# Streaming-encoder block on one core: embedding blocks at three stage borders, a gate unit moved ahead of attention, and attention's last pair handed over in SBUF

## The chip, the cores and the metric

The kernel runs on one core of one Trainium2 chip. The metric is the time of one execution in device microseconds (us). The engines of a core have their own instruction queues, each worked through in order: PE (TensorE, the matmuls; its weight loads are listed as PEld), DVE (VectorE, elementwise), ACT (ScalarE, activation functions and copies), POOL (GpSimd) and SP (SyncE). SP, POOL and ACT also issue DMA transfers; these are listed as SPq, POOLq and ACTq.

## The reference

One layer of an encoder over 512 tokens of width 2048, in float32:

```python
h = rms_norm(x)
q_a, k_a, v_a, q_g, k_g, v_g, r_g, gate_lr = split(h @ w_in)        # 2048 -> 6160
y_a = chunked_band_attention(q_a, k_a, v_a, bias)                   # 16 heads of 64
o_g = rms_norm(gated_linear_attention(q_g, k_g, v_g, log_a(gate_lr)))   # 4 heads, value width 256
x = x + concat(y_a, o_g * silu(r_g)) @ w_out                        # 2048 -> 2048
h = rms_norm(x)
u_gate, u_val = split(causal_conv3(h @ w_ffn_up))                   # 2048 -> 2 x 5632
x = x + (gelu(u_gate) * u_val) @ w_ffn_down
h = rms_norm(x)
x = x + sigmoid(h @ w_ple_gate) * (p @ w_ple_proj)                  # p: 512 x 256 embeddings
return rms_norm(x)
```

## The kernel before

Each large matrix product is made with seven block products in place of eight (P1 to P7, a fast matrix multiplication with sums of weight blocks and sums of input blocks). A **unit** is one piece of such a product: 256 output columns, 512 tokens. A block product is 24 matmuls of 128 x 128 x 256: every operand is split into a high and a low part, and high x high, high x low and low x high are added up in PSUM. The high part of a weight block is a copy on ACT, the low part a subtraction on DVE (`prep_high`, `prep_low`, tile `wsplit`); both are issued two products ahead of their use. After each product `collect` takes the result out of PSUM, on ACT for the first product of a quarter of the unit's output and on DVE otherwise.

The **stages** run one after the other: `linear` (units 16 to 19 are the four heads of linear attention, 20 to 23 the attention's values, 8 a gate unit), `front` (units 0 to 7 are pairs of attention heads, 9, 10 and 11 the other gate units), `embed` (four blocks of p @ w_ple_proj), `wo` (x @ w_out), `up`, `dn0` to `dn2` (the down projection in three parts) and `pg` (the gate of the embeddings). `wo`, `up` and `pg` begin and end with two units side by side, so that their products alternate. A step is one product; an embedding block is one step too, of 24 matmuls with 512 columns (`embedding`, L722). It goes through four PSUM results from auxiliary banks (`psum_aux`; four such banks at first, two from `more_banks` on), which ACT copies into two pages `pp_o`; the ACT queue stores each page, 512 KB, to the scratch `ppd`. The gate stage reads it back hundreds of steps later (`load_gate`).

The order of the work on PE, DVE and ACT is written out by hand. The list `agenda` holds for every step what is to be issued there, with a key: 0 ahead of everything, 1 between the high and the low part of the coming weights, above 1 behind the matmuls of the step. What a unit's output needs after its last product is such a list as well (`attend`, `after_gates`, `gla_head`: pairs of step and key, counted from the step behind the unit). These instructions stay in program order on their engines, so an instruction that waits holds up all behind it.

A stage's input operands lie in SBUF in seven forms (R11, R21, R22, N1, T3, N2, T4), each in two tiles of four blocks (`g` 0 and 1). They come from scratch in DRAM (`store_pair` writes them, `Stage.load` reads them) and are split again. The last two blocks of a **chained** stage come straight from SBUF, as `tails`: for `wo` those of gate units 10 and 11, for `up` and `pg` those of the last two units of the stage before.

Raw weights are loaded into pages of 512 KB. `free` lists the free ones and `wanted` the blocks to come, in order; `issue` gives free pages to wanted blocks, oldest page first. A name with a star is a page that the kernel will write itself: `issue` leaves one page free for it and goes on; `made_page` takes it. `release` puts a page back and calls `issue` at once. S blocks are sums: SP loads one block and POOL adds the other with an accumulating DMA. Other pages have fixed tags and turn in small rings (`page`): `c` (c0, and later c1, c2, c0), `x` (r6, later x0 and x1), `u`. Page r7 holds in turn the output of a linear head (`og`) and then the attention's bias.

Linear attention's own tiles (pool `gla`) and the attention's (pool `att`) share space: `open_attention` closes the first and opens the second, nine steps after unit 0 begins. `attention_done` opens the pool `late`, gives three more pages to the weights, and switches the rings; it comes 19 steps after unit 7 begins.

Of the kernel before, what the change touches and what calls it, by code (L numbers as in the profile page):

```python
# [43 lines left out]
def encoder_block(ctx: ExitStack, tc: tile.TileContext, A, out):  # L44
# [677 lines left out]
    def embedding(unit):  # L722

        hi, lo = unit.w["PP"]
        for i in range(4):
            if i % 2 == 0:
                spare = {(0, 2): (pg, "u0"), (1, 2): (late[0], "u3")}.get((unit.u, i))
                o = (spare[0].tile([P, 1024], F32, tag=spare[1], name="pp_o") if spare else page("c", "pp_o")).rearrange("p (s t) -> p s t", s=2)
            pp = psum_aux("pp")
            for k in range(2):  # L730
                w = slice((i * 2 + k) * P, (i * 2 + k + 1) * P)
                product3(pp, hi[:, w], lo[:, w], ps_[0][:, k], k == 0, k == 1)
            act.activation(o[:, i % 2, :], pp, AF.Copy)
            if i % 2:
                m = 4 * unit.u + i - 1
                nc.scalar.dma_start(ppd[m % 8:m % 8 + 2, m // 8].rearrange("m p t -> p m t"), o)

# [5 lines left out]
    def attend(unit):  # L743
# [97 lines left out]
        if b % 2:  # L841
            items.append((12, 1, lambda: store_pair(mixd, b // 2, ypair[0][:, 0, :], ypair[0][:, 1, :])))
# [220 lines left out]
    def front_weights(u, q):  # L1063
# [3 lines left out]
        if u >= 16:  # L1067
# [4 lines left out]
    linear = Stage("in", [16, 20, 21, 17, 22, 23, 18, 8, 19], 8, None, front_weights, front_after, "own", "own", single=True,  # L1072
                   groups=((0,), (1, 2), (3,), (4, 5), (6,), (7,), (8,)))
    front = Stage("in", [0, 1, 2, 3, 4, 5, 6, 7, 9, 10, 11], 8, None, front_weights, front_after, "dma", "dma", single=True)
# [8 lines left out]
    embed = Stage("pp", [0, 1, 2, 3], 8, None, lambda u, q: A["w_ple_proj"][u], lambda u: [], "dma", "dma", single=True)  # L1083
    for u in embed.units:
# [13 lines left out]
    units = [u for st in stages for u in st.units]  # L1098
    steps = []
    base = {}  # L1100
    for st in stages:
        for group in st.groups:
# [4 lines left out]
            need = [[(u, name) for name in (NEEDS[u.sums] if u.stage is not embed else ("L11",))] for u in group]  # L1107
# [47 lines left out]
    agenda[i0 + 2].append((0, lambda: raws.update(p=embedding_load(page("c", "pT")))))  # L1155
# [16 lines left out]
    agenda[i0 + 11].append((0, more_banks))  # L1172
# [169 lines left out]
    agenda[base[front.units[0]] + 9].append((1.5, open_attention))  # L1342
# [138 lines left out]
def _layout(x, p, norm_mix_w, w_in, att_rel_bias, w_gla_gate_up, b_gla_gate, gla_norm_w,  # L1481
# [16 lines left out]
        "w_out": _blocks(w_out[0].reshape(8, 2, P, D).transpose(1, 0, 2, 3).reshape(D, D)),  # L1498
# [31 lines left out]
```

## Time and profile before

| what | value |
|---|---|
| median of 3 runs | 2252.64 us (2250.53 to 2253.16) |
| the profiled execution | 2254.49 us |
| its span on the core | 2252.8 us |
| mean granted TensorE clock | 0.993 |
| matmuls | 18588 |
| DMA moved | 518.31 MB |

The span is the time from the first to the last instruction of the profiled execution; some time lies around it. In a row of the timeline stand the start and the length in us, the engine, the line, the operation, the tile written and the tiles read, the shape, the number of such instructions merged, and in brackets the idle time of the engine before it with what ended it. Because a helper records most instructions, their line is L64, and they are told apart by their tiles: `wsplit` is a split weight, `accA` to `accC` are PSUM results of products, `u` a unit's output, `pp_o` and `pp` an embedding block's page and PSUM result, `in_`, `wo_`, `up_`, `dn_` and `pg_` with R, N or T the operands of the stages. DMA rows show the issue; a transfer's time to landing is listed apart.

### The profile page before, as it was taken

The numbers are of one execution on the slowest core, as the hardware profiler recorded it, in microseconds if no ns is written. First come the engines' busy times: TensorE is split into PE (matmuls) and PEld (weight loads), VectorE is DVE, ScalarE is ACT, GpSimd is POOL, SyncE is SP. The second block draws the span as 40 slices with busy tenths as digits, with TensorE's granted clock in tenths as the row PEclk, the third lists the DMA queues.
The fourth block names the chain that finished last, engine by engine and source line by source line (L and its number), as shares of the span: only waits on it lengthen the run. The fifth ranks groups of instructions, "written<-read, shape, count | busy, mean of one in ns | idle before, by whom it ended". The sixth has DMA issues, their size and how long they took to land.

```text
span 2252.8 us, 46290 instructions
## 1 busy us (share of the span) xinstructions
PE 2196.4 (97%) x18588; PEld 2146.3 (95%) x18588; DVE 1937.3 (86%) x2655; ACT 1344.6 (60%) x2000; POOL 158.6 (7%) x196
## 2 busy tenths in 40 slices
PE   9999998999999999999999999999999999999995
PEld 7899988999989999999999999999999999999995
DVE  8476778999879898999889888988898797999997
ACT  9455556777666665555555555555564554667655
POOL 0000000000000100000000001000000100000000
PEclk9999999999999999999999999999999999999998
DMA  6466755667888987888888888888876967879894
GB/s 238 134 181 193 214 160 150 180 189 199 287 268 278 315 235 207 224 229 218 221 218 223 211 225 216 222 218 213 256 237 232 314 229 260 299 252 336 264 307 152
DMA packets 190760, 518.31 MB, mean 230 GB/s; under 512 B 20272, under 2 KB 66608, under 8 KB 190544
## 3 DMA queue, kind: packets, MB, share of 16 engines
q1 hardware_dynamic: 160272, 415.72, 54.2%
q0 software_dynamic: 25920, 93.33, 23.2%
q10 hardware_dynamic: 4352, 6.29, 0.8%
q8 instruction: 146, 2.39, 0.4%
q14 instruction: 70, 0.57, 0.1%
HBM read 441.86 MB, written 71.30 MB: 228 GB/s over the span
## 4 chain that ended last, share of the span: by engine, by line
PE 80%; DVE 9%; DMA 4%; ACT 4%; issue 2%; ACTq 0%; SPq 0%; DVEq 0%
PE accA L64 41%; PE accC L64 21%; PE accB L64 10%; DVE wsplit L64 3%; PE v L240 1%; PE v L239 1%; PE v L241 1%; ACT wsplit L64 1%; DVE u L64 1%; DMA dn_R<-g_R 1%; PE py L64 1%; PE ptr L64 1%; PE psc L64 1%; DMA ppd<-pp_o 1%; DVE l L64 1%
## 5 line engine op out<-in xcount | busy, mean ns | idle before, releaser
L64 ACT ACTIVATE wsplit<-l 128x1024 fp32r<-128x1024 f32 (+1 forms) x476 | 495.7, 1042 | 292.0 <-PE accC L64 123.6
L64 DVE TENSOR_TENSOR wsplit<-l,wsplit 128x1024 fp32r<-128x1024 f32 (+1 forms) x476 | 570.5, 1200 | 114.7 <-ACT wsplit L64 113.3
L64 DVE TENSOR_TENSOR wsplit<-s,wsplit 128x1024 fp32r<-128x1024 f32 (+1 forms) x253 | 303.4, 1200 | 58.2 <-ACT wsplit L64 57.7
L64 ACT ACTIVATE wsplit<-s 128x1024 fp32r<-128x1024 f32 (+1 forms) x253 | 262.7, 1039 | 64.0 <-PE accB L64 36.1
L64 ACT ACTIVATE u<-accA 128x256 f32<-128x256 f32 x302 | 114.2, 378 | 268.9 <-PE accA L64 268.9
L64 PE MATMUL accA<-up_T,wsplit 128*128 128x256 f32 x2112 | 253.6, 276 | 0.4 <-ACT wsplit L64 0.4
L64 PEld LDWEIGHTS accA<-up_T,wsplit 128*128 128x128 f32 x2112 | 245.8, 188 | 0.7 <-ACT wsplit L64 0.6
L64 DVE SCALAR_TENSOR_TENSOR cv<-u,cw,cv 128x511 f32<-128x511 f32 (+1 forms) x176 | 131.5, 747 | 3.1
L405 POOL DMA_DIRECT2D s<-in_w_up x88 | 76.2, 866 | 764.2 <-DMA s<-in_w_up 280.9
L64 PE MATMUL accA<-up_N,wsplit 128*128 128x256 f32 x1056 | 127.1, 276 | 1.3 <-DVE wsplit L64 1.3
L64 PE MATMUL accA<-dn_T,wsplit 128*128 128x256 f32 x1056 | 126.2, 276 | 2.0 <-DVE wsplit L64 1.7
L64 PE MATMUL accC<-up_N,wsplit 128*128 128x256 f32 x1056 | 126.8, 276 | 0.9 <-DVE wsplit L64 0.9
L64 PE MATMUL accB<-up_R,wsplit 128*128 128x256 f32 x1056 | 126.8, 276 | 0.6 <-DVE wsplit L64 0.6
L64 PE MATMUL accA<-up_R,wsplit 128*128 128x256 f32 x1056 | 126.9, 276 | 0.0
L64 PE MATMUL accC<-up_R,wsplit 128*128 128x256 f32 x1056 | 126.5, 276 | 0.0
L64 PEld LDWEIGHTS accA<-dn_T,wsplit 128*128 128x128 f32 x1056 | 122.5, 188 | 2.5 <-DVE wsplit L64 2.1
L64 PEld LDWEIGHTS accA<-up_N,wsplit 128*128 128x128 f32 x1056 | 123.0, 188 | 1.6 <-DVE wsplit L64 1.6
L64 PEld LDWEIGHTS accC<-up_N,wsplit 128*128 128x128 f32 x1056 | 122.9, 188 | 1.1 <-DVE wsplit L64 1.1
L64 PEld LDWEIGHTS accB<-up_R,wsplit 128*128 128x128 f32 x1056 | 122.9, 188 | 0.8 <-DVE wsplit L64 0.8
L64 PEld LDWEIGHTS accA<-up_R,wsplit 128*128 128x128 f32 x1056 | 122.9, 188 | 0.5 <-issue 0.5
L64 PEld LDWEIGHTS accC<-up_R,wsplit 128*128 128x128 f32 x1056 | 122.8, 188 | 0.0
L64 PE MATMUL accA<-in_T,wsplit 128*128 128x256 f32 x768 | 97.6, 284 | 8.0 <-DVE u L64 4.7
(337 smaller groups left out, 4235.8 us busy)
## 6 DMA issues: line engine op xcount, KB each, us to landing
l<-in_w_up SPq DMA_DIRECT2D x132, 512.0 KB, 4.6
s<-in_w_up SPq DMA_DIRECT2D x88, 512.0 KB, 5.0
s<-in_w_up POOLq DMA_DIRECT2D x88, 512.0 KB, 6.7
l<-in_w_dn SPq DMA_DIRECT2D x56, 448.0 KB, 5.6
l<-in_w_blk SPq DMA_DIRECT2D x48, 512.0 KB, 4.7
s<-in_w_blk SPq DMA_DIRECT2D x32, 512.0 KB, 4.4
s<-in_w_blk POOLq DMA_DIRECT2D x32, 512.0 KB, 7.3
l<-in_w_out SPq DMA_DIRECT2D x28, 512.0 KB, 5.1
```

The source lines that it names most:

```text
L64: ins = f(*args, **kw)
L239: nc.tensor.matmul(ps[t], x[:, 0, sl], wh, start=kt == 0, stop=False)
L240: nc.tensor.matmul(ps[t], x[:, 0, sl], wl, start=False, stop=False)
L241: nc.tensor.matmul(ps[t], x[:, 1, sl], wh, start=False, stop=kt == KD - 1)
L405: nc.gpsimd.dma_start(t, src("L22" if name == "S1" else "L11"), accum_op=ALU.add)
```

## The change

- Gate unit 9 moves from `front` (behind attention unit 7) to the end of `linear` (behind head 19). `open_attention` is one step earlier. The last step of the two early gate units' output work (product with the head's output, then the pair's differences and stores) moves from steps 1 and 1 to steps 4 and 5 behind the unit; for unit 11 all of it is in the first step behind it. The page rings of the loaded heads change accordingly.
- The operands of `wo` have a new block order: attention pairs 0 to 2, gate units 8, 9, 10, then attention's last pair, then unit 11; the rows of `w_out` are reordered in the inputs to match. Attention's last pair (unit 7) is not stored to DRAM any more but is `tails[0]`; unit 10 is stored and read back. The loads and splits of `wo` are at other steps.
- Two embedding blocks stay ahead of `wo`, the third stands between `wo` and `up`, the fourth between `dn2` and `pg`. For these two the embeddings `p` are loaded and split again, into the tile of T3 group 1, and their two output pages are weight pages (`O0*` and `O1*` in `wanted`). The later operand splits of `up` and `pg` are one step later.

```diff
@@ embedding
         for i in range(4):
             if i % 2 == 0:
-                spare = {(0, 2): (pg, "u0"), (1, 2): (late[0], "u3")}.get((unit.u, i))
-                o = (spare[0].tile([P, 1024], F32, tag=spare[1], name="pp_o") if spare else page("c", "pp_o")).rearrange("p (s t) -> p s t", s=2)
+                o = (PP_PAGES[unit.u, i]() if unit.u < 2 else made_page(unit, f"O{i // 2}")).rearrange("p (s t) -> p s t", s=2)
...
                 nc.scalar.dma_start(ppd[m % 8:m % 8 + 2, m // 8].rearrange("m p t -> p m t"), o)
+                if unit.u >= 2:
+                    release(unit.tag[f"O{i // 2}"])
@@ attend
         if b % 2:
-            items.append((12, 1, lambda: store_pair(mixd, b // 2, ypair[0][:, 0, :], ypair[0][:, 1, :])))
+            items.append((12, 1, lambda: store_pair(mixd, b // 2, ypair[0][:, 0, :], ypair[0][:, 1, :])) if b < 7 else
+                         (12, 6, lambda: tails.__setitem__(0, store_pair(None, 0, ypair[0][:, 0, :], ypair[0][:, 1, :]))))
@@ load_heads, after_gates
-        unit.M = {"on": page("x" if g < 2 else "c", "on").rearrange("p (s t) -> p s t", s=2)}
+        unit.M = {"on": page("x" if g < 3 else "c", "on").rearrange("p (s t) -> p s t", s=2)}
...
-            ops = store_pair(mixd if g < 2 else None, 4 + g, unit.o[:, 0, :], unit.o[:, 1, :])
-            if g >= 2:
-                tails[g - 2] = ops
+            ops = store_pair(mixd if g < 3 else None, 3 + g, unit.o[:, 0, :], unit.o[:, 1, :])
+            if g == 3:
+                tails[1] = ops
...
-                (0, 2, lambda: act.activation(unit.o, unit.o, AF.Silu)), (1, 1, times), (1, 3, pair)]
+                (0, 2, lambda: act.activation(unit.o, unit.o, AF.Silu))] + (
+                    [(4, 1, times), (5, 1, pair)] if g < 2 else [(1, 1, times), (1, 3, pair)] if g == 2 else
+                    [(0, 3, times), (0, 4, pair)])
@@ stages
-    linear = Stage("in", [16, 20, 21, 17, 22, 23, 18, 8, 19], 8, ...
-    front = Stage("in", [0, 1, 2, 3, 4, 5, 6, 7, 9, 10, 11], 8, ...
-    embed = Stage("pp", [0, 1, 2, 3], 8, ...
+    linear = Stage("in", [16, 20, 21, 17, 22, 23, 18, 8, 19, 9], 8, ...
+    front = Stage("in", [0, 1, 2, 3, 4, 5, 6, 7, 10, 11], 8, ...
+    embed, embed_up, embed_pg = (Stage("pp", us, 8, None, lambda u, q: A["w_ple_proj"][u], lambda u: [], "dma", "dma", single=True)
+                                 for us in ([0, 1], [2], [3]))
...
+    pp_tile = lambda pool, tag: pool.tile([P, 1024], F32, tag=tag, name="pp_o")
+    PP_PAGES = {(0, 0): lambda: pp_tile(late[0], "c2"), (0, 2): lambda: pp_tile(pg, "u1"),
+                (1, 0): lambda: pp_tile(late[0], "c1"), (1, 2): lambda: pp_tile(late[0], "c2")}
+    sequence = stages[:4] + [embed_up] + stages[4:8] + [embed_pg] + stages[8:]
...
-            need = [[(u, name) for name in (NEEDS[u.sums] if u.stage is not embed else ("L11",))] for u in group]
+            need = [[(u, name) for name in (NEEDS[u.sums] if u.kind != "pp" else ("L11",) if u.u < 2 else ("O0*", "O1*", "L11"))] for u in group]
@@ borders
+                if b.chained and (op, g) == ("T3", 1):
+                    start, at = 16, 19
+                elif b.chained and at > 15:
+                    at += 1
...
+        if b.chained:
+            agenda[i0 + 7].append((0, lambda: raws.update(p=embedding_load(page("c", "pT")))))
+            agenda[i0 + 11].append((1, lambda: embedding_split(raws["p"], xtile("T3", 1, "ps"))))
...
-                agenda[base[u] + (3, 3, 6, 3)[u.u - 8]].append((0, lambda u=u: load_heads(u)))
+                agenda[base[u] + (3, 3, 3, 6)[u.u - 8]].append((0, lambda u=u: load_heads(u)))
...
-            agenda[i0 + (14 if kept else n + 1)].append((0, lambda op=op, g=g: wo.load(op, g)))
-            agenda[i0 + (16 if kept else n + 4)].append((3, lambda op=op, g=g: wo.split(op, g, True, (0,) if g else ())))
-        at, k = ((9, 1), (9, 1), (10, 1), (12, 1), (16, 3), (14, 3), (15, 3))[n]
+            agenda[i0 + (11 if kept else n + 1 + g)].append((0, lambda op=op, g=g: wo.load(op, g)))
+            agenda[i0 + (13 if kept else n + 5)].append((3, lambda op=op, g=g: wo.split(op, g, True, ())))
+        at = (7, 7, 8, 9, 13, 10, 11)[n]
+        agenda[i0 + at].append((3.5, lambda op=op: wo.split(op, 1, False, (0,))))
+        at, k = ((8, 1), (8, 1), (9, 1), (10, 1), (13, 3.6), (12, 3), (13, 3.6))[n]
         agenda[i0 + at].append((k, lambda op=op: wo.split(op, 1, False, (1,))))
...
-    agenda[i0 + 2].append((0, lambda: raws.update(p=embedding_load(page("c", "pT")))))
+    agenda[i0 + 2].append((0, lambda: raws.update(p=embedding_load(pg.tile([P, 1024], F32, tag="r7", name="pT")))))
...
-    agenda[i0 + 11].append((0, more_banks))
+    agenda[i0 + 9].append((0, more_banks))
...
-    agenda[base[front.units[0]] + 9].append((1.5, open_attention))
+    agenda[base[front.units[0]] + 8].append((1.5, open_attention))
```

Here `i0` is the first step of the last unit, or of the last pair, ahead of the border.

More of the change, by code (lines that the diff above doesn't have):

```diff
@@ L1070, in front_weights @@
         return A["w_blk"][j, int(q[2]) - 1]
[L1072 to L1074 removed]
+    linear = Stage("in", [16, 20, 21, 17, 22, 23, 18, 8, 19, 9], 8, None, front_weights, front_after, "own", "own", single=True,
+                   groups=((0,), (1, 2), (3,), (4, 5), (6,), (7,), (8,), (9,)))
+    front = Stage("in", [0, 1, 2, 3, 4, 5, 6, 7, 10, 11], 8, None, front_weights, front_after, "dma", "dma", single=True)
     linear.x = front.x
@@ L1082, in encoder_block @@
                 u.banks = u.lead.banks
-    embed = Stage("pp", [0, 1, 2, 3], 8, None, lambda u, q: A["w_ple_proj"][u], lambda u: [], "dma", "dma", single=True)
-    for u in embed.units:
+    embed, embed_up, embed_pg = (Stage("pp", us, 8, None, lambda u, q: A["w_ple_proj"][u], lambda u: [], "dma", "dma", single=True)
+                                 for us in ([0, 1], [2], [3]))
+    for u in embed.units + embed_up.units + embed_pg.units:
         u.order, u.uses, u.made, u.kind = ("PP",), dict(L11=1), set(), "pp"
@@ L1097, in encoder_block @@
     wo = stages[3]
-    units = [u for st in stages for u in st.units]
+    pp_tile = lambda pool, tag: pool.tile([P, 1024], F32, tag=tag, name="pp_o")
+    PP_PAGES = {(0, 0): lambda: pp_tile(late[0], "c2"), (0, 2): lambda: pp_tile(pg, "u1"),
+                (1, 0): lambda: pp_tile(late[0], "c1"), (1, 2): lambda: pp_tile(late[0], "c2")}
+    sequence = stages[:4] + [embed_up] + stages[4:8] + [embed_pg] + stages[8:]
+    units = [u for st in sequence for u in st.units]
     steps = []
     base = {}
-    for st in stages:
+    for st in sequence:
         for group in st.groups:
```

2 lines of the change are left out of this document (1 added, 1 removed).

## The prediction

> **What bounds the kernel now.** I read the page's busy table first, then stretches of the span, then the timeline wherever TensorE (PE) had idle time.
>
> ```profile
> span 2252.8 us, 46290 instructions
> PE 2196.4 (97%) x18588; PEld 2146.3 (95%) x18588; DVE 1937.3 (86%) x2655; ACT 1344.6 (60%) x2000; POOL 158.6 (7%) x196
> ```
>
> PE is idle for only 2252.8 - 2196.4 = 56.4 us, and no matmul is added or removed by the change: the same embedding blocks and gate units run at other places. So the time can move only by idle time, and by matmuls that run at the half clock after a long idle. The stretches that hold the places touched (columns: length, then busy us of PE, PEld, DVE, ACT, POOL, then granted clock, DMA share, GB/s):
>
> ```profile
> 350.00:400.00 50.00, 43.27 (x355) 41.37 (x354) 41.78 (x87) 29.07 (x56) 3.46 (x4) 0.93 0.68 185
> ...
> 790.00:800.00 10.00, 10.00 (x90) 10.00 (x90) 9.79 (x16) 8.38 (x17) 0.86 (x1) 1.00 1.06 271
> 800.00:810.00 10.00, 8.18 (x67) 7.59 (x66) 10.00 (x15) 8.15 (x14) 0.00 (x0) 1.00 0.79 274
> 810.00:820.00 10.00, 8.71 (x75) 8.31 (x74) 9.43 (x12) 5.29 (x10) 0.86 (x1) 1.00 0.61 202
> ...
> 2060.00:2070.00 10.00, 9.43 (x78) 8.90 (x77) 9.40 (x15) 8.06 (x14) 2.18 (x3) 1.00 1.06 298
> 2070.00:2080.00 10.00, 8.33 (x67) 7.58 (x65) 10.00 (x13) 8.14 (x15) 0.44 (x1) 1.00 1.04 313
> 2080.00:2090.00 10.00, 8.97 (x76) 8.78 (x77) 9.43 (x15) 5.28 (x11) 0.00 (x0) 1.00 0.89 334
> ```
>
> Four places matter. A: where the linear heads end and attention begins (300 to 372). B: where the output stage begins (609 to 649). C: the up stage's first pair, where PE loses 1.82 + 1.29 = 3.1 us with DVE full. D: the gate stage's first pair, 0.57 + 1.67 + 1.03 = 3.3 us lost in the same manner.
>
> **A, the gate unit behind the last head.** The timeline (start, length, engine, line, operation, idle before it):
>
> ```profile
> 301.31 0.76 DVE L64 TENSOR_TENSOR tp<-u 128x256 f32<-128x256 f32 x2
> 301.98 0.88 DVE L64 SCALAR_TENSOR_TENSOR tp<-tp,u 128x256 f32<-128x256 f32 x2
> ...
> 306.84 1.24 PE L64 MATMUL accA<-in_T,wsplit 128*128 128x256 f32 x8 [2.90 <-DVE wsplit L64]
> 307.90 4.50 PE L64 MATMUL accC<-in_R,wsplit 128*128 128x256 f32 x24
> 312.23 2.88 PE L64 MATMUL accA<-in_T,wsplit 128*128 128x256 f32 x24
> ...
> 353.79 0.33 SPq L1046 DMA_DIRECT2D ond<-og  x1
> 358.21 1.03 SPq L754 DMA_DIRECT2D bias<-in_bias  x2
> 360.43 1.19 PE L64 MATMUL accC<-in_R,wsplit 128*128 128x256 f32 x8 [2.04 <-DVE wsplit L64]
> 365.48 0.17 DVE L64 MEMSET bias<- 64x128 f32 x1 [5.11 <-DMA bias<-in_bias]
> 367.24 5.46 PE L64 MATMUL accA<-in_T,wsplit 128*128 128x256 f32 x24 [4.70 <-DVE u L64]
> ```
>
> The bias of the first attention unit shares page r7 with the last head's output, so its load waits for that output's store, the mask waits for the load, and DVE, which works in order, lets PE run dry. With seven products of unit 9 between that head and attention, head 19's store is issued four steps into unit 0 and the bias load ten steps in: six products of about 2.9 us lie between, against a store of about 4.4 us (358.21 - 353.79). Unit 9's own seven stores and its load of the head's output go through SP there with it, past no operand load that is due. I count the wait as gone: 2.04 + 4.70 + (5.46 - 2.88) = 9.3 us. Unit 8's product and pair also move three or four steps later; the four `tp` instructions (0.76 + 0.88, about 1.5 us net) leave the DVE queue ahead of the operand that PE awaited for 2.90 us. That idle should fall to about 1.4 us, and the slow matmuls behind it (4.50 for 2.88) go: about 3.2 us gained. But the moved instructions, the gate's multiply too, land in a stretch where DVE has no idle either; I give back 1.2 us. A comes to +11.3 us. Bounds: +8 if the new neighbour stalls like unit 19 did, +13 if nothing is given back.
>
> **C and D, one embedding block each.** The block needs nothing of the stage's last results, so it should cover DVE's lateness: at most 3.1 and 3.3 us. What it brings: two extra loads and splits of the embeddings (1.04 us ACT and 1.22 us DVE each, as the 1024-column rows further down), and output pages taken from the weight pages. Here the code shows a wait. Two pages are reserved (`O0*`, `O1*`). Block half 0 takes one; after its store is issued the page is released and `issue()` runs at once: one reservation is left, two pages are free, so the older free page goes to the next weight, and `O1` gets the page just released. Half 1's first eviction, an ACT instruction, must therefore wait until half 0's store has landed. The same reuse is seen before:
>
> ```profile
> 614.87 1.07 ACT L64 ACTIVATE pp_o<-pp 128x512 f32<-128x512 f32 x2
> 615.97 0.38 ACTq L736 DMA_DIRECT2D ppd<-pp_o  x1
> ...
> 626.33 1.09 ACT L64 ACTIVATE pp_o<-pp 128x512 f32<-128x512 f32 x2 [3.59 <-DMA ppd<-pp_o]
> ...
> DMA to landing us min/median/max: 5.0/9.0/14.5
> ppd<-pp_o ACTq DMA_DIRECT2D x1, 512.0 KB, 9.9
> ```
>
> The median is over all eight stores, half of them queued behind their twin. The one that counts has no twin ahead of it; the first such store took 9.9, the shortest of all 5.0. I take 8 us, nearer the long end, since DMA is full at both places (shares 1.06 from 790 and from 2060). What stands behind the waiting eviction on ACT is seen where C lies now:
>
> ```profile
> 790.16 5.60 PE L64 MATMUL accA<-up_R,wsplit 128*128 128x256 f32 x48
> 793.21 1.05 ACT L64 ACTIVATE wsplit<-l 128x1024 fp32r<-128x1024 f32 x1
> 794.34 0.51 ACT L64 ACTIVATE u<-xs,cols 128x256 f32<-128x256 f32 x1
> 794.75 0.62 ACT L64 ACTIVATE up_R<-up_R 128x512 fp32r<-128x512 f32 x1
> 795.28 0.71 ACT L64 ACTIVATE up_R<-u 128x256 fp32r<-128x256 f32 x2
> 795.89 1.04 ACT L64 ACTIVATE up_N<-up_N 128x1024 fp32r<-128x1024 f32 x1
> 797.10 1.05 ACT L64 ACTIVATE wsplit<-l 128x1024 fp32r<-128x1024 f32 x1
> ...
> 2060.50 4.70 PE L64 MATMUL accA<-pg_R,wsplit 128*128 128x256 f32 x40
> 2065.23 1.05 ACT L64 ACTIVATE wsplit<-l 128x1024 fp32r<-128x1024 f32 x1
> ```
>
> First, ACT is late already: at C the weight split ahead of the block's evictions ends 4.1 us after PE begins the step, at D 5.8. The block's four quarters use two auxiliary banks by then, so the third quarter, which PE reaches at 2.8 us (half of 5.63, a block's row below), waits for the first eviction: until 4.1 + 0.54 at C, 5.8 + 0.54 at D, some 0.6 later for the added split. Loss 2.4 at C, 4.1 at D. Second, from the end of eviction 1, PE has 2.3 us of the block and 5.60 us of the first pair left, 7.9 us. ACT needs 0.4 for the store's issue, 8 for the landing, then 1.07 (two evictions) + 0.4 + 0.51 + 0.62 + 0.71 + 1.04 + 1.05 = 5.4 us up to the weight split that the second product needs. PE is idle for 0.4 + 8 + 5.4 - 7.9 = 5.9 us. Third, idle of that size costs a slow product: 5.46 - 2.88 = 2.6 us more. With 0.5 us for what DVE still owes, C costs 2.4 + 5.9 + 2.6 + 0.5 = 11.4 in place of 3.1, -8.3 us; D 13.1 in place of 3.3, -9.8 us. With 5.0 us for the landing the idle is 2.9 and the slow matmuls 4.50 - 2.88 = 1.6: -4.3 and -5.8. With 9.9 it is 7.8: -10.2 and -11.7. SP also waits, for half 1's store, before it loads a weight into that page; behind it stand the last operand loads, due four to nine products later. I count no time for that; if they come too late it is part of the lower bound.
>
> The Trainium skill, "TensorE: Matmul & The Clock Gate", "Part 1: The HAM clock gate", says that PE falls to half its clock after about one idle window of 3.4 us; by it the 5.9 us idle is charged, and an idle of 2.9 us may or may not be. The trace has slow matmuls behind 4.70 us and behind 2.90 us.
>
> **B, two blocks instead of four.** Rows around the border:
>
> ```profile
> 608.90 5.63 PE L64 MATMUL pp<-ps,wsplit 128*128 128x512 f32 x24
> 610.33 0.41 DVE L64 TENSOR_TENSOR u<-u,accC 128x256 f32<-128x256 f32 x1
> 615.04 1.22 DVE L64 TENSOR_TENSOR u<-u,rb 128x1024 f32<-128x1024 f32 x1
> 617.99 1.06 ACT L64 ACTIVATE u<-u 128x1024 f32<-128x1024 f32 x1 [0.44 <-ACT pp_o L64]
> 629.77 0.70 ACT L64 ACTIVATE wo_R<-u 128x256 fp32r<-128x256 f32 x2
> 636.58 5.62 PE L64 MATMUL accA<-wo_R,wsplit 128*128 128x256 f32 x48
> 648.72 5.60 PE L64 MATMUL accA<-wo_N,wsplit 128*128 128x256 f32 x48
> ```
>
> From the first block to the third pair of products pass 39.8 us; four blocks and two pairs are 4 x 5.63 + 2 x 5.62 = 33.8, so 6.0 are lost. After, two blocks give 11.3 us of cover for unit 11's chain: DVE's backlog, multiply by the norm 1.22, Silu 1.06 behind the block's evictions, multiply 1.22, operand bodies and attention's tails, split. DVE's backlog at 608.90 is about 4 us (the collection at 610.33 is of a product that ended near 606); attention's last items now run five steps into unit 11 and bring about 2 us more. In DVE's order: backlog 6, multiply 1.2, weight split 1.2, one operand's bodies 1.8 (1.22, and some 0.6 for 512 columns, between 1.22 for 1024 and 0.41 for 256), multiply 1.2, two tails 0.8, the pair's differences 1.6 (as `tp` above), two tails 0.8: 14.6, and handovers of about 1 us: 16 against 11.3, 4.7 us idle, some 2.3 for slow matmuls or later waits. That is 7.0 against 6.0: -1 us. Past the queues: attention's end, and with it three weight pages and the `conv` load, moves from two steps ahead of unit 11 to five steps into it, so the first output pair's weights are issued on SP and POOL some 5 to 9 steps ahead of their splits where it was 8 to 11 (counted through the page lists of the code); and unit 10's operands now pass through DRAM with one step between store and load. Both are in the lower bound, -6. The reordered rows of `w_out` are the same loads and cost nothing. The upper bound, +4, has the chain nearly covered.
>
> **Sum.** +11.3 - 1 - 8.3 - 9.8 = -7.8 us, a slowdown: the profiled execution's 2254.49 (span 2252.8 and 1.7 around it) becomes 2262.3. It stands 1.85 above the median of the runs shown, 2252.64, so a run should show 2260. The terms' bounds give 13 + 4 - 4.3 - 5.8 = 6.9 us faster to 8 - 6 - 10.2 - 11.7 = 19.9 us slower: 2246 to 2273.
>
> **Rivals.** Faster, 2237 (chance 0.17): half 1 finds another page, or ACT's wait is over before PE has used the block and the first pair; then C and D give 2.6 and 2.8, A 11.3, B -1: 15.7 us less. It decides from a landing of about 2 us downward; against it stands the shortest, 5.0. Short landing, 2252 (0.18): the lone store lands in 5.0 us, and 11.3 - 1 - 4.3 - 5.8 is +0.2. For it speaks that each of the eight stores had loads of other queues and mostly a twin to share with. The Trainium skill, "DMA: Bandwidth & Descriptors", "Queues, rings and completion order", has each DMA engine take turns between queues packet by packet, so that a store alone on ACT's queue would not stand behind SP's backlog; by that rule this rival gains. Attention's wait stays in another form, 2269 (0.08): A gives 2 only; the six steps speak against it. Front border, 2268 (0.12): B costs 9, for DVE's backlog and late operands. The forecast has 0.45.
>
> Faster by over 0.2% (4.5 us, about what these runs can tell from no change) is the first rival, a quarter of the second and a tenth of the forecast's spread: 0.27. Within 0.2%: the rest of the second and some of the forecast, 0.20. Slower: 0.53. The likeliest case's own range is 2246 to 2273; over all cases I reach down to 2241 and stop at 2272, which leaves out most of the first rival and little above.
>
> **What would show it.** Right: after, `pp_o` evictions with an idle of 5 to 8 us put down to `ppd<-pp_o` at two places, one just ahead of the up stage and one ahead of the gate stage, PE idle there just behind the first pair put down to ACT or DVE, slow matmuls after; no idle of 5 us before the bias memset, and clock 1.00 around 360. Wrong: PE idle under 2 us at C and D; or no such wait on ACT; or the clock dip at attention's start still there.

## The result, and the profile after

The changed kernel takes 2276.34 us (median; 2274.66 to 2281.99), the kernel before, timed beside it on the same chip, 2251.59 (2250.37 to 2253.16). The ratio is 1.0114 with a 95% interval of 1.0095 to 1.0133: 24.75 us slower, about three times the 7.8 us of the forecast and outside its range. The profiled execution after took 2281.99 us, the longest of those timed; the one before took 2254.49. The two traces therefore differ by 27.5 us of span, and the terms further down add up to that.

The busy table of the kernel after:

```profile
span 2280.3 us, 46295 instructions
PE 2203.8 (97%) x18588; PEld 2153.5 (94%) x18588; DVE 1939.8 (85%) x2657; ACT 1347.5 (59%) x2003; POOL 158.7 (7%) x196
```

The matmuls are as many as before, busy for 7.4 us longer (2203.8 - 2196.4); the other 20.1 us are idle time of PE (2280.3 - 2203.8 = 76.5 us in place of 56.4).

The timeline of the kernel after where the third block now stands, ahead of the up stage (start, length, engine, operation, idle before it):

```profile
782.68 0.63 PE L64 MATMUL pp<-ps,wsplit 128*128 128x512 f32 x2
...
789.15 3.06 PE L64 MATMUL pp<-ps,wsplit 128*128 128x512 f32 x12 [2.76 <-ACT o L64]
789.62 0.37 ACTq L735 DMA_DIRECT2D ppd<-o  x1
...
792.04 5.62 PE L64 MATMUL accA<-up_R,wsplit 128*128 128x256 f32 x48
...
802.12 1.08 ACT L64 ACTIVATE o<-pp 128x512 f32<-128x512 f32 x2 [12.53 <-DMA ppd<-o]
...
804.71 0.69 DVE L64 TENSOR_TENSOR up_R<-up_R 128x512 fp32r<-128x512 f32 x1 [14.84 <-ACT up_R L64]
...
807.23 7.96 PE L64 MATMUL accB<-up_R,wsplit 128*128 128x256 f32 x48 [9.57 <-ACT wsplit L64]
```

ACT issues the first half's store at 789.62 and stands still for 12.53 us, until it has landed, before it may write the second half (802.12). Behind it wait the operands and the weight split of the second product, DVE for 14.84 us, and PE for 9.57; the product that then comes takes 7.96 us in place of 5.60. Inside the block PE has already waited 2.76 us for an auxiliary bank. At the gate stage it is the same:

```profile
2070.97 0.63 PE L64 MATMUL pp<-ps,wsplit 128*128 128x512 f32 x2
2073.29 2.56 PE L64 MATMUL pp<-ps,wsplit 128*128 128x512 f32 x10 [1.69 <-DVE wsplit L64]
2078.61 4.49 PE L64 MATMUL pp<-ps,wsplit 128*128 128x512 f32 x12 [2.75 <-ACT o L64]
2079.07 0.37 ACTq L735 DMA_DIRECT2D ppd<-o  x1
2082.93 5.62 PE L64 MATMUL accA<-pg_R,wsplit 128*128 128x256 f32 x48
2091.34 1.08 ACT L64 ACTIVATE o<-pp 128x512 f32<-128x512 f32 x2 [12.29 <-DMA ppd<-o]
...
2096.45 8.46 PE L64 MATMUL accB<-pg_R,wsplit 128*128 128x256 f32 x48 [7.90 <-ACT wsplit L64]
```

To price each part I cut both traces at the starts of the same products: B from the first embedding block to the end of the output stage's products, C from there to a product 40 steps into the up stage, D from the end of the down stage to a product 24 steps into the gate stage. In C and D of the kernel after, the moved block comes first. Stretches of the kernel before, then of the kernel after (length, busy time of PE, PEld, DVE, ACT and POOL, granted clock, DMA share, GB/s):

```profile
608.90:790.16 181.26, 175.58 (x1443) 170.13 (x1441) 150.02 (x192) 111.56 (x167) 13.00 (x15) 1.00 0.92 293
790.16:906.64 116.48, 112.79 (x973) 110.81 (x971) 103.16 (x135) 72.45 (x108) 9.54 (x11) 1.00 0.82 227
2060.50:2134.95 74.45, 70.16 (x589) 67.65 (x587) 69.69 (x95) 51.22 (x80) 7.81 (x9) 1.00 0.93 283
```

```profile
610.79:782.68 171.89, 165.30 (x1394) 162.12 (x1393) 150.58 (x197) 107.04 (x160) 10.42 (x12) 1.00 0.90 292
782.68:916.69 134.01, 120.04 (x996) 117.10 (x995) 105.75 (x137) 77.50 (x116) 12.14 (x14) 0.96 0.78 214
2070.97:2162.18 91.21, 77.93 (x612) 74.96 (x611) 72.13 (x99) 54.62 (x85) 8.68 (x10) 0.93 0.81 248
```

A block without a wait takes 5.46 us (half of the 10.91 from the first block at 610.79 to the output stage at 621.70). B lacks two blocks now, C and D have one more:

| part | worked out from the rows | forecast | measured in the traces |
|---|---|---|---|
| A, up to the first block | 608.90 against 610.79 | +11.3 | -1.9 |
| B | 181.26 against 171.89 + 10.91 | -1 | -1.5 |
| C | 116.48 against 134.01 - 5.46 | -8.3 | -12.1 |
| D | 74.45 against 91.21 - 5.46 | -9.8 | -11.3 |
| sum | | -7.8 | -26.8 |

The other 0.7 of the 27.5 us lie between C and D (0.4) and behind D (0.3). C and D came in the way that was forecast and cost more; A, which was to gain more than either costs, gained nothing in these two traces.

### The profile page after: what moved, and what is told of

It is laid out like the page before. It is cut to its first block, busy times and chain, and to the rows that moved or that the text cites. A ratio compares the mean times of both kernels' runs of the same rounds, so it can differ in the third digit from the quotient of the medians.

```text
span 2280.3 us, 46295 instructions
## 1 busy us (share of the span) xinstructions
PE 2203.8 (97%) x18588; PEld 2153.5 (94%) x18588; DVE 1939.8 (85%) x2657; ACT 1347.5 (59%) x2003; POOL 158.7 (7%) x196
## 4 chain that ended last, share of the span: by engine, by line
PE 79%; DVE 9%; DMA 5%; ACT 3%; issue 2%; ACTq 0%; SPq 0%; DVEq 0%; POOLq 0%
PE accA L64 40%; PE accC L64 21%; PE accB L64 10%; DVE wsplit L64 3%; DMA s<-in_w_blk 1%; PE v L239 1%; PE v L240 1%; PE v L241 1%; DMA ppd<-o 1%; DVE u L64 1%; ACT wsplit L64 1%; PE ptr L64 1%; PE py L64 1%; DMA s<-in_w_ple_gate 1%; DVE l L64 1%
## 5 line engine op out<-in xcount | busy, mean ns | idle before, releaser
L64 DVE TENSOR_TENSOR l<-l,l 128x1024 f32<-128x1024 f32 (+1 forms) x86 | 102.7, 1194 | 0.1
```

Source lines behind the costliest of these rows:

```text
L64: ins = f(*args, **kw)
```

## The experiments

Times are medians, each beside the kernel before on the same chip (2252.69 to 2253.04 in the three groups of runs). Diffs are against the kernel after unless another is named.

**The page that is still being stored (own_pages).**

```diff
+            if i == 0 and unit.u >= 2:
+                own = [made_page(unit, f"O{n}") for n in range(2)]
             if i % 2 == 0:
-                o = (... if unit.u < 2 else made_page(unit, f"O{i // 2}"))...
+                o = (... if unit.u < 2 else own[i // 2])...
```

> Both output pages of a moved block are taken ahead of its first eviction, so that the second half no longer gets the page the first half just gave back; all else as in the kernel after. Theory 1 (the wait for the first half's store is what costs at the up and gate borders): ACT's idles of 12.53 and 12.29 us put down to ppd<-o vanish, PE's idles of 9.57 and 7.90 us behind the first pair go, and the slow products behind them (7.96 and 8.46 in place of 5.60) too: up to 22.7 us less, 2254 to 2258 us. Theory 2 (ACT, DVE and DMA are late there anyway, the store only ends last): another wait, by ACT's backlog or by weights that SP loads late, takes most of its place, and no more than 10 us come back: 2266 us or more. PE's idle of 2.75 us inside each block, which waits for an auxiliary bank, stays in both.

Measured: 2259.72 us, ratio 1.0038 (1.0024 to 1.0051), so 7.0 us more than the kernel before beside it, where the kernel after took 24.75 more. The median is 16.6 us below that of the kernel after. In the rows of the two moved blocks ACT waits for no store any more. The stretches C and D of this run:

```profile
780.19:903.83 123.64, 118.04 (x996) 114.94 (x995) 105.76 (x137) 77.66 (x116) 10.90 (x13) 1.00 0.83 227
2057.01:2139.96 82.95, 75.96 (x613) 72.49 (x611) 72.41 (x100) 54.80 (x85) 8.68 (x10) 0.98 0.91 278
```

C fell by 10.4 us and D by 8.3. Against the kernel before, less a block's 5.46, 1.7 and 3.0 are left. The time misses the first theory's 2254 to 2258 by 1.7 us and is far from the second's 2266: the reuse of the page was the main cost. SP still waits for such stores before it loads weights into those pages (5.8 and 1.6 us at C, 7.8 and 2.7 at D). That costs little: in the first pair of units of both stages PE's idles are between 0.26 and 1.15 us, each put down to DVE.

**The banks (own_pages_and_banks).** As own_pages, and:

```diff
-            pp = psum_aux("pp")
+            tag, pp = bank("pp") if unit.u >= 2 and i >= 2 else (None, psum_aux("pp"))
...
             act.activation(o[:, i % 2, :], pp, AF.Copy)
+            if tag:
+                banks.append(tag)
```

> As own_pages, and the second half of each moved block also takes two of the accumulator banks that are free at that point, in place of the two auxiliary banks that its first half still holds. Theory 1 (what is left of the moved blocks' cost, 1.7 us at up and 3.1 at the gate stage by the segment times of own_pages, is PE waiting 2.77 and 2.72 us for ACT to empty an auxiliary bank): both idles inside the blocks go, nothing takes their place since ACT's evictions are then 2.7 us further from the next weight split, and the time falls by 4 to 5.5 us from 2259.7, to 2254 to 2256. Rival (ACT's and DVE's backlog only moves: the weight split behind the evictions becomes what PE waits for): the idle shows up behind the first pair, and the time stays within 1.5 us of 2259.7.

Measured: 2254.97 us, ratio 1.0010 (1.0001 to 1.0019), 4.75 us less than own_pages and within the first theory's 2254 to 2256. It is 1.9 us more than the kernel before beside it. The same stretches:

```profile
776.62:898.52 121.90, 117.98 (x997) 115.07 (x996) 105.74 (x137) 77.48 (x116) 11.35 (x14) 1.00 0.85 232
2052.23:2131.57 79.34, 74.29 (x613) 71.50 (x611) 72.14 (x99) 54.63 (x85) 8.67 (x10) 1.00 0.94 289
```

Less a block, C is 116.4 and D 73.9, against 116.48 and 74.45 before the change. The run combined, further down, has the same edit; there C is 116.4 and D 74.4. So a moved block now costs nothing at either place, and gains between 0.1 and 0.6 us at D. The gain that the prediction's first rival counted on (2.6 and 2.8 us, from covering DVE's lateness) isn't there even without the waits.

**The size of the store (half_stores, first_store_128_kb).** In the first, each eviction has its own store of 256 KB:

```diff
             act.activation(o[:, i % 2, :], pp, AF.Copy)
+            if unit.u >= 2:
+                m = 4 * unit.u + i
+                nc.scalar.dma_start(ppd[m % 8, m // 8], o[:, i % 2, :])
```

> The kernel after, where each of a moved block's four evictions is followed by a store of its own, 256 KB, in place of one store of 512 KB behind every second; the pages and their reuse stay. Theory 1 (the landing of 12.4 us was a transfer sharing full DMA with the loads of the other queues, so it goes with the bytes): ACT issues the first half store 0.6 us earlier, each lands in 6 to 8 us, the wait ahead of the third eviction falls from 12.5 to 6 to 8 us at both places, and the kernel takes 8 to 13 us less than 2276. Rival (the landing is mostly a fixed latency, or a place in a line of earlier descriptors): the landing stays at 10 to 12 us, the wait at 10 us or more, and the kernel within 4 us of 2276.

Measured: 2276.79 us. ACT's two waits:

```profile
796.53 0.60 ACT L64 ACTIVATE o<-pp 128x512 f32<-128x512 f32 x1 [8.92 <-DMA ppd<-o]
...
2085.31 0.60 ACT L64 ACTIVATE o<-pp 128x512 f32<-128x512 f32 x1 [11.77 <-DMA ppd<-o]
```

The waits miss the 6 to 8 us, and the time misses the gain of 8 to 13: it is what the rival forecast. The waits can't tell the two theories apart, though. The page is free only when both stores have landed (787.64 + 8.8 = 796.44 us at C, ahead of the eviction at 796.53), as many bytes as before, of which the first half set out a microsecond earlier. The landings say more: the first half stores landed after 8.1 us at C and 8.4 at D, where 512 KB took 12.4 and 12.2, and the second half stores, each behind its twin, after 8.8 and 11.6. The next run takes the bytes away:

```diff
-                nc.scalar.dma_start(ppd[...].rearrange("m p t -> p m t"), o)
+                c = slice(0, 32 if unit.u >= 2 and i == 1 else P)
+                nc.scalar.dma_start(ppd[...].rearrange("m p t -> p m t")[c], o[c])
+                for n in (0, 4) if unit.u == 1 and i == 3 else ():
+                    nc.scalar.dma_start(ppd[n:n + 2, 1].rearrange("m p t -> p m t")[32:], o[32:])
```

> The kernel after, but the first store of each moved block carries 32 of the 128 partitions, 128 KB in 64 pieces of 2 KB, in place of 512 KB in 256; the other 96 partitions of that part of the scratch are written from another block's page at the front border, so two blocks' embeddings are wrong in those rows. half_stores didn't tell what it was made for, since the third eviction waits for both half stores and so for as many bytes as before. Theory 1 (the landing is the pieces' turns at full DMA): a quarter of the pieces lands in 3 to 6 us, ACT's wait of 12.53 and 12.29 us falls to 3 to 6, PE's idles of 9.57 and 7.90 us to 0 to 3, and the kernel takes 12 to 20 us less than 2276. Rival (a fixed latency of this queue under load): a landing of 10 us or more, ACT's wait too, and the time within 4 us of 2276.

Measured: 2271.84 us, 4.5 less than the kernel after and not the 12 to 20 that were expected. By the traces the stretches C and D are 6.2 and 5.5 us shorter than in the kernel after, and the extra stores at the front border cost 5.2 us there (177.1 us for B's stretch in place of 171.9). ACT and PE at the two places:

```profile
800.88 1.09 ACT L64 ACTIVATE o<-pp 128x512 f32<-128x512 f32 x2 [6.38 <-DMA ppd<-o]
...
806.02 4.80 PE L64 MATMUL accB<-up_R,wsplit 128*128 128x256 f32 x40 [1.88 <-ACT wsplit L64]
...
2083.50 1.09 ACT L64 ACTIVATE o<-pp 128x512 f32<-128x512 f32 x2 [6.38 <-DMA ppd<-o]
...
2088.63 7.32 PE L64 MATMUL accB<-pg_R,wsplit 128*128 128x256 f32 x48 [3.48 <-ACT wsplit L64]
```

The wait is 6.38 us at both places, a little over the 3 to 6 expected, and half of what it was in the kernel after. The landing grows with the size of the store, though a quarter of the bytes still takes half the time; the rival's fixed latency of 10 us or more is excluded.

Size is not all of it. The edits of unit8_steps_1_1 and unit0_five_pages (further down) leave the moved blocks as they are. ACT's wait there is 12.64 us at D in the first run, and 12.22 and 12.39 at the two places in the second, but 8.67 at C in the first run, where the store landed after 8.6 us. The landing also goes with what the other queues move meanwhile; the last section has the numbers.

**The gate unit alone (four_ahead_of_wo, gate_unit_alone).** All four blocks ahead of `wo` again; the second run adds pages that are free in time, the old step for the extra banks, and attention's tails split two steps later:

```diff
-    embed, embed_up, embed_pg = (Stage("pp", us, ...) for us in ([0, 1], [2], [3]))
+    embed = Stage("pp", [0, 1, 2, 3], 8, ...)
...
-    agenda[i0 + 9].append((0, more_banks))
+    agenda[i0 + 11].append((0, more_banks))
```

> The kernel after with all four embedding blocks ahead of the output stage again (pages c2, u1, c1, u3, then c2, u1, c1, c2); the moved gate unit and the SBUF pair stay. Theory 1 (the two moved blocks cost 13.6 and 11.3 us, the gate unit 1.9, by the two traces): the first block begins at 610.8 us as in the kernel after, the idle ahead of up and pg is that of the kernel before, and four blocks give the border at least the 6.0 us loss it had, at most none: 2247 to 2254 us. The prediction's term for the gate unit (11.3 us gained) would give 2240 us. Theory 3 (the parts disturb each other through the page lists): over 2258 us.

> The gate unit's move and the SBUF pair alone: the kernel after with four blocks ahead of wo, each with a page that no store in flight still holds (c2, u1, c1, u3, u2, c2, u1, c1), the two extra accumulator banks handed over two steps later as before the change, and attention's tails split two steps later. Theory 1 (the bias wait of 9 us did go, but the waits that took its place cost as much, 1.9 us more in the profile): the time is within 3 us of the kernel before, 2250 to 2256. The prediction's term (11.3 us gained) gives 2241 us. Rival (in the run four_ahead_of_wo it was the order of the tails' splits and the banks at the border that hid a gain of the front): 2244 to 2248 us.

Measured: 2257.10 (1.0017, 1.0007 to 1.0027) and 2253.77 us (1.0004, 0.9995 to 1.0013). The first lies in no theory's window; PE had 4.75 us of idle ahead of its third block, for evictions that ACT reached late, and in the second run 3.09 at the same place. The second is what its first theory forecast: in it the gate unit's move and the SBUF pair, with the border that they bring, are worth between a gain of 1.1 and a loss of 2.9 us. In its trace the first block begins 1.5 us earlier than before the change (607.41 against 608.90), and the border from there to the up stage is 1.3 us longer (182.56 against 181.26). The 11.3 of the forecast are excluded.

**What took the gain of the front (unit8_steps_1_1, gate_unit_alone_unit8_early, unit0_five_pages, combined).** The edits:

```diff
# unit8_steps_1_1; also on top of gate_unit_alone, and in combined
-                    [(4, 1, times), (5, 1, pair)] if g < 2 else [(1, 1, times), (1, 3, pair)] if g == 2 else
+                    [(1, 1, times), (1, 3, pair)] if g < 3 else
# unit0_five_pages
+    front.units[0].sums = "own"
# combined: own_pages_and_banks, the first edit, and
-                (8, 1, rooted), (8, 3, root_exact), (9, 1, result),
+                (8, 1, rooted), (8, 3, root_exact), (9, 3 if hd == 3 else 1, result),
```

> The kernel after, but with the two early gate units' multiply and pair at steps 1 and 1 behind the unit, as before the change. Theory 1 (unit 8's product and pair, moved three to four steps later, land in a stretch where DVE has no slack and cost 3.1 us there): the first embedding block begins 2 to 3 us earlier than at 610.79, about 2273 us in all. Rival (the stretch is full of DVE work with or without these, so that the place doesn't matter): within 1 us of 610.79, with the idle back at one place, 2.9 us ahead of the product at 307. A second rival: the stall of the first operand returns and costs more than the four now seen (0.72, 1.52, 1.23, 1.41 us): later than 612.

> The kernel after, but attention unit 0 makes its sum S2 in the page of L11, as the linear heads do, and so needs five weight pages where it needed six; the number of operations stays. Theory 1 (weight pages are short when unit 0 follows the gate unit with no attention matmuls beside it, so its sums are loaded too late: the idles of 1.00, 1.08 and 2.52 us from 372 to 398): the sums' loads are issued some 3 us earlier, most of these idles go, and the first embedding block begins 3 to 4 us earlier than at 610.79. Rival (the loads are late by DMA's share of the stretch or by the queues' order, not for want of a page): within 1 us of 610.79 and the idles stay.

> As gate_unit_alone, with the two early gate units' multiply and pair back at steps 1 and 1 behind the unit. In the run unit8_steps_1_1 the first embedding block began at 606.46 us against 610.79, 608.29 and 614.17 in three profiles with steps 4 and 5. Theory 1 (the later steps cost about 3 us): 2 to 4 us less than gate_unit_alone, and less than the kernel before: 2247 to 2250 us. Rival (the difference between those profiles is spread from run to run): within 1 us of gate_unit_alone.

> own_pages_and_banks with two changes to the front: the early gate units' multiply and pair at steps 1 and 1 again, and the last linear head's final scaling (two DVE instructions, 1.41 us) behind the coming weights' split in place of ahead of it. By step times, the products from the 60th to the 69th took 40.46 us with the gate items early, 41.44 to 43.0 with them late (before the change 40.3), and unit 0, alone now, took 21.4 where unit 11 alone took 19.4 before the change; in unit 0 PE waits 1.45 us for a weight split that DVE makes right behind that scaling. Theory 1 (these are losses of DVE's order): products 60 to 69 in 40.5 us, unit 0 in 20 to 20.5, in sum 2 to 3 us less than own_pages_and_banks's 2254.97, so 2252 to 2253, no better than the kernel before by what can be told. Rival (DVE is full over the stretch, and the idle comes back two or three products later): within 1 us of 2255, with the loss moved into units 1 and 2.

Measured: 2277.55, 2275.95, 2255.01 and 2254.99 us, each within what can't be told from the kernel that it was built on (2276.34, 2276.34, 2253.77, 2254.97). In unit8_steps_1_1 the first block did begin 4.3 us earlier than in the kernel after (606.46), but the profiled execution was the fastest of its four, and the median is no better. gate_unit_alone_unit8_early lies 1.2 us above gate_unit_alone, in neither theory's window and far from the gain. In unit0_five_pages the first block begins at 609.08, between its two theories, and unit 0 still takes 21.4 us, so it is not a page that it lacks. In combined the products from the 60th to the 69th took 40.3 us as expected, but unit 0 took 21.75, not the 20 to 20.5 expected, and unit 1 grew from 22.91 to 25.28: the rival was right, the loss moved on. The runs show where the gain of the front went; since none of these orders won, they don't show which of the instructions there would have to go.

The places are seen when the front is cut by units. Before: the last head's last three products, unit 0, unit 1, unit 2, and unit 11, which had no other work of PE beside it:

```profile
301.85:314.95 13.10, 10.20 (x72) 10.00 (x73) 12.96 (x22) 7.34 (x10) 0.92 (x2) 0.87 0.75 203
314.95:342.17 27.22, 27.22 (x226) 26.07 (x225) 19.57 (x24) 11.43 (x17) 1.73 (x2) 1.00 0.69 174
342.17:373.31 31.14, 24.41 (x178) 23.34 (x177) 23.23 (x36) 17.56 (x27) 1.73 (x2) 0.89 0.58 161
373.31:400.36 27.05, 27.05 (x245) 25.98 (x245) 24.25 (x57) 19.38 (x41) 1.73 (x2) 1.00 0.64 167
...
589.51:608.90 19.39, 19.30 (x170) 19.14 (x169) 18.88 (x22) 15.02 (x20) 0.00 (x0) 1.00 1.01 361
```

After: the same three products, then gate unit 9, unit 0 (the one that now stands alone), unit 1, unit 2; and the same five in own_pages_and_banks, whose front has the same instructions:

```profile
302.14:314.90 12.76, 9.11 (x73) 8.55 (x73) 12.66 (x18) 7.35 (x10) 0.86 (x1) 1.00 0.95 234
314.90:345.12 30.22, 28.98 (x227) 27.52 (x225) 21.02 (x29) 11.44 (x17) 1.73 (x2) 0.94 0.62 176
345.12:366.54 21.42, 20.36 (x171) 19.85 (x169) 16.83 (x22) 14.14 (x17) 0.86 (x1) 1.00 0.43 128
366.54:389.88 23.34, 21.27 (x178) 20.70 (x177) 16.81 (x20) 11.86 (x17) 2.60 (x3) 1.00 0.90 249
389.88:421.31 31.43, 28.91 (x246) 27.53 (x246) 28.45 (x68) 20.83 (x43) 1.73 (x2) 0.95 0.68 170
```

```profile
301.27:314.03 12.76, 9.10 (x73) 8.54 (x74) 12.66 (x18) 7.35 (x10) 0.86 (x1) 1.00 0.94 235
314.03:342.74 28.71, 27.48 (x226) 26.16 (x225) 21.01 (x29) 11.42 (x17) 1.72 (x2) 1.00 0.68 185
342.74:364.15 21.41, 19.96 (x171) 19.44 (x170) 16.83 (x22) 14.14 (x17) 1.18 (x2) 1.00 0.46 131
364.15:387.06 22.91, 21.29 (x179) 20.72 (x178) 18.13 (x22) 11.85 (x17) 2.27 (x3) 1.00 0.92 256
387.06:415.56 28.50, 28.05 (x246) 26.10 (x246) 27.36 (x67) 21.11 (x46) 1.72 (x2) 1.00 0.70 186
```

Unit 1, which held the bias wait, gained 7.8 and 8.2 us (31.14 against 23.34 and 22.91). Against that stand, in the kernel after and in own_pages_and_banks: the last head's three products and the unit behind them, together 2.7 and 1.2 us longer; the unit that stands alone, 2.0 longer in both (21.42 and 21.41 against unit 11's 19.39); unit 2, 4.4 and 1.5 longer. In all -1.3 and +3.6 us. Seven profiles have these same front instructions (the two above, own_pages, half_stores, first_store_128_kb, four_ahead_of_wo and gate_unit_alone). Over the seven, unit 1 gains 7.8 to 8.4 us and the unit that stands alone loses 2.0 each time; the first two stretches lose 1.1 to 2.7 and unit 2 loses 1.4 to 4.9.

In the kernel after, PE in the last head's three products and in gate unit 9, then DVE where attention's bias mask is made:

```profile
305.68 1.18 PE L64 MATMUL accA<-in_T,wsplit 128*128 128x256 f32 x8 [1.41 <-DVE wsplit L64]
...
309.40 1.18 PE L64 MATMUL accC<-in_R,wsplit 128*128 128x256 f32 x8 [0.72 <-DVE wsplit L64]
312.09 2.97 PE L64 MATMUL accA<-in_T,wsplit 128*128 128x256 f32 x24 [1.51 <-DVE u L64]
...
324.73 4.22 PE L64 MATMUL accA<-in_N,wsplit 128*128 128x256 f32 x24
...
383.76 0.17 DVE L64 MEMSET bias<- 64x128 f32 x1
```

The mask's row has no idle ahead of it any more. The idle of 2.90 us fell to 1.41, as forecast, but idles of 0.72 and 1.51 us came behind it. The second of them waits for a collection (311.53) that DVE reaches behind the moved multiply of unit 8 (`u<-u,on`, 309.26, 1.22 us long). In gate unit 9 another idle, 1.24 us at 321.73, comes ahead of a slow product, 4.22 us where the like one took 3.01 before. With the multiply and the pair at their old steps (the three runs that have them there) the same ten products take 40.3 to 40.5 us, in the seven profiles 41.5 to 43.0. So their late place does cost 1.0 to 2.7 us; but when they are put back, the loss comes in unit 0 or unit 1.

Inside the unit that stands alone PE waits for DVE; of gate_unit_alone:

```profile
357.97 1.19 PE L64 MATMUL accA<-in_T,wsplit 128*128 128x256 f32 x8 [1.45 <-DVE wsplit L64]
```

## Why the prediction was wrong

- **A, the bias wait: right.** 9.3 us were forecast; the unit that held them gained 7.8 to 8.2 in the two traces shown, and no wait ahead of the mask is left.
- **A, the rest: wrong, and the larger of the two errors.** Two steps of it failed. "I give back 1.2 us" priced the gate unit's late multiply and pair against a gain of 3.2 and made +2.0 of them. The idle that was to shrink did shrink to the 1.4 us forecast, but the late instructions brought new idles behind it, and the stretches show -1.2 to -2.7. And the sum had no term for the new neighbours: with unit 9 moved, the seven products of unit 0 run with no attention beside them and take 2.0 us longer than the like products of unit 11 did, and unit 2 pays another 1.5 to 4.4. The bound of +8 fell for the same reason: it asked whether one neighbour stalls, and the losses came in four stretches. By the timed run gate_unit_alone, A and the border that it brings are worth about -0.7 us together (1.1 gained to 2.9 lost). The rival "attention's wait stays in another form" (A gives 2; 2269, chance 0.08) comes nearest in A's size, but not in its mechanism, since the wait did go.
- **B: right in size.** -1.5 against -1. The idle that was foreseen ahead of the output stage came as several waits for operands and weight splits, of 0.84 to 1.65 us each, in its first three pairs of products, and not as one. B took within 0.1 us of 171.9 in every trace with two blocks there and their stores unchanged, but the kernel before has one trace only.
- **C and D: mechanism right, landing mis-sized.** The page given back and drawn again, the wait on ACT and the bank all came as read from the code. The landing was taken as 8 us, with 9.9 as the upper bound; in the kernel after it took 12.4 and 12.2. With 12.4 the forecast's own formula gives an idle of 0.4 + 12.4 + 5.4 - 7.9 = 10.3; measured were 9.57 and 7.90. At D the second half of the block ran slowly (4.49 us for 12 matmuls that take 2.7 at 5.46 a block), which covered 1.8 us more. The bank stall, 2.4 and 4.1, was 2.76 and 2.75; the slow product, 2.6, was 2.36 and 2.86 (7.96 and 8.46 less 5.60). In unit8_steps_1_1, where the store at C landed after 8.6 us, C cost 8.2 us where 8.3 were forecast, though its parts differ there too (an idle of 4.15 us, not 5.9). The step that failed is the choice of the landing's rows: "nearer the long end, since DMA is full at both places". DMA was just as full at the front border, where the first store took 9.9 us (its queues' shares add up to 1.05), but there the accumulating loads had 27% of the engines' time, and at C and D 63 and 66%.
- **The range.** Its slow end rests on a gain of 8 in A and a landing of 9.9 us at most. Both bounds were passed, so the time lies beyond it.

Put together from the timed runs, each beside its kernel before: of 24.75 us, own_pages leaves 7.0 and the banks 1.9. These 1.9 (0.2 to 4.3) are A and B, less the little that D gains.

## What to carry to other kernels

When a page goes back into a pool in the same breath as the store that reads it is issued, look up who takes the next page: an in-order engine that draws it again waits for its own store, and all behind it waits too; here an edit of three lines that draws both pages first gave back 16.6 of 24.75 us. And when a piece of matmul work is taken from one place to cover a wait at another, price the place that it leaves and each unit whose neighbours change, not the wait alone.

## What the runs showed of the hardware

How long a lone store on ACT's queue takes to land goes with its size and with what the other queues move meanwhile. The DMA queues of the kernel after from 785 to 803 us (packets, MB, share of the 16 engines' time; q0 carries the accumulating loads that POOL issues, q1 what SP issues, q10 this store), and the store's issue (KB, us to landing):

```profile
q0 software_dynamic: 575, 2.10, 60.1%
q1 hardware_dynamic: 818, 2.46, 36.8%
q10 hardware_dynamic: 272, 0.52, 7.6%
...
ppd<-o ACTq DMA_DIRECT2D x1, 512.0 KB, 12.4
```

The same for single stores, with q0's share from the issue to the landing:

| store | KB | q0's share | landing, us |
|---|---|---|---|
| kernel after, C, second half (803.23) | 512 | 0 | 2.8 |
| unit8_steps_1_1, C, first half | 512 | 39.6% | 8.6 |
| kernel after, C, first half | 512 | 62.9% | 12.4 |
| kernel after, D, first half | 512 | 65.6% | 12.2 |
| half_stores, first store at C and at D | 256 | 58.4%, 65.9% | 8.1, 8.4 |
| first_store_128_kb, first half at C and at D | 128 | 56.9%, 69.9% | 6.3, 6.3 |

The sizes were set by experiments. What the other queues moved was not; that part is a comparison of traces.

By an estimate from the shares, one packet costs an engine 0.601 x 18 x 16 / 575 = 0.30 us on q0, 0.13 on q1 and 0.08 on q10, 0.51 for a turn of all three. A store of 512 KB is 256 packets of 2 KB, 16 for each engine, one of 128 KB is 4: twelve turns fewer, 6.1 us by this estimate, and the landing fell from 12.4 and 12.2 to 6.3. Some 4 us of each of these landings are not in the turns, and no run here shows what they are; with q0 at rest (and q1 at 3.9%) the whole landing took 2.8 us. The Trainium skill, "DMA: Bandwidth & Descriptors", "Queues, rings and completion order", says that an engine takes turns between queues packet by packet. The difference between the sizes agrees with that, if a packet is what the profile counts as one. But the conclusion that the prediction drew for its rival, that such a store is hardly held up, doesn't follow: by the estimate each of its packets waits for one of every other queue, and the accumulating loads' are the longest.

The same front instructions also don't take the same time in each run: the first block began between 604.70 and 614.17 us in the seven profiles named above. One difference between them is where a slow product falls. In gate_unit_alone it lies in the last head's three products, which take 14.17 us at a granted clock of 0.88; in the kernel after they have nearly the same idles, take 12.76 us at clock 1.00, and the slow product lies in the unit behind them. The Trainium skill, "TensorE: Matmul & The Clock Gate", "Part 1: The HAM clock gate", has the gate's window run free of the kernel's start. That would make this a matter of where an idle falls in the window; no run here sets that place, so it isn't shown. Two of these profiles can differ by up to 9.5 us at the first block, so a smaller change of this front can't be read from one pair of them; the gain of unit 1 and the 2.0 us of the unit that stands alone are the parts that all seven repeat.
